# Second-half projections in 512-column passes, with some stores issued by ScalarE

## The chip, the cores and the metric

The kernel runs on one core of one Trainium2 chip. A core has a matrix engine (TensorE, PE in the profile), VectorE (DVE), ScalarE (ACT), GpSimd (POOL) and SyncE (SP). Each has its own instruction queue and works through it in order. In this kernel SP issues every DMA: loads at line 235, stores at line 240. The metric is the device time of one execution in microseconds; the kernel before takes 1905.05 us, the median of three runs (1902.53 to 1905.58).

## The reference

One layer of a streaming encoder works on 2048 prompt frames and 64 sample frames of width 1024. All arithmetic is float32.

```python
h = rmsnorm(x, norm_g) @ w_in            # 1024 -> 6144 columns
qa, ka, va, za, qb, kb, vb, zb, ga, gb = jnp.split(h, _split_points(), axis=-1)
# branch A: differential attention, 4 heads, q and k in two 64-wide halves, 128-wide values
s = einsum(q, k) / 8 - slope * |q_pos - k_pos|, masked to chunks of 64 up to the query's own
p = softmax(s);  a = p[:, :, 0] - lam * p[:, :, 1];  oa = a @ v
# branch B: retention, 4 heads, 128-wide, a decaying state carried from chunk to chunk
o = (q k^T * decay inside the chunk) v + q r * decay;  r = decay_c * r + k^T v * zeta
# merge
m = ga * ((rmsnorm(oa) * silu(za)) @ w_oa) + gb * ((rmsnorm(ob) * silu(zb)) @ w_ob)
y = x + m @ w_out
```

The outputs are y, the normalised attention keys, the attention values and the final retention states. The sample frames run the same layer against a cache of 4096 past frames.

## The kernel before

**Precision.** Each float32 operand is split into a high part, rounded to TensorE's fp32r type, and a low part, the rest. A product takes three fp32r matmuls: high by high, high by low, low by high. ScalarE makes the high part by a copy, POOL or VectorE the low part by a subtraction.

**Two halves of the prompt.** The projection runs first over frames 0 to 1023 and the sample frames, then over frames 1024 to 2047 (`half` 0 and 1). Its parts come in two kinds. A *natural* part (`natural`) keeps a tile of 128 frames stationary and streams weight columns past it; the output has frames in its partitions. The queries, keys and values of attention (`qa`, `ka`, `va`) and the values of retention (`vb`) are made so. A *transposed* part (`transposed`) keeps 128 weight columns stationary and streams frames. Retention's queries and keys (`qb`, `kb`) and the gates (`za`, `zb`, `ga`, `gb`) are made so, in the first half by a seven-product Strassen scheme (`strassen`, line 848). All plain projection matmuls stand in `mm_group`, line 998.

**Wide and narrow.** In the first half the natural parts take 512 weight columns at once (`wide`): 8 pieces of 128 x 512. In the second half each takes two passes of 256 columns: 4 pieces of 128 x 2 x 256 a pass, and two frame tiles share one PSUM bank of 512 columns. A piece is staged in a `ws` buffer, cast by ScalarE (line 952) and its low part taken by POOL (line 962); high and low parts sit in 12 places of tag `w`, each 128 x 512 floats.

**After each group** a finisher takes the bank. `fin_va` has ScalarE cast the high part into `thi` (one buffer, line 1246) and copy the raw values into `ev` (three, line 1248), and VectorE make the low part in `tlo` (two, line 1250); the three are stored. `fin_qk` normalises, transposes on PE and stores. `fin_vb` copies and stores. `fin_t`, for a transposed group, copies into `ev` and calls `put`, which stores. Every store goes through `st` and so to SP's queue.

**Order of the work.** A planner in the kernel's own Python runs generators as tasks. Each has a priority and yields the time at which it can go on, by a cost model (`P`, `A`, `V`, `G`, `ld`, `st`). When PE is free in the model the first ready task in order of priority issues its next instructions. The program order of TensorE, ScalarE and VectorE is the order so made. Attention and retention (`z_stream`) come before the projection (`w_stream`), which fills what they leave.

In the second half the parts come in this order before the change: first pass of va, of ka, of qa, a mark `kqv0`, the second passes, a mark `kqv1`, vb in two passes, then qb and kb in two units each, a mark `ret`, then the gates. While they run, attention works on the first half and then, its loads allowed by the marks, on the second. Per pair of query blocks it makes scores (`qk_block`, matmuls at lines 1517 and 1518, VectorE's bias and minimum at 1526), exponentials (ScalarE, 1557), the difference (VectorE, 1579), and then transposes the weights (1629), splits them (1642, 1644) and multiplies by the values (1607 to 1609). Scores lie in a row arena, one tile of `LATER` = 12032 columns for both halves, which retention shares. `load_head` and `load_q` issue the loads of keys, values and queries.

When both streams are done the output stage runs: branch projections (line 2306 on) and the final product (line 2430 on). Its weights and gated branch outputs are prepared from the moment attention ends.

Of the kernel before, what the change touches and what calls it, by code (L numbers as in the profile page):

```python
# [39 lines left out]
LAT = 250.0  # L40
SLACK = 400.0
# [8 lines left out]
LATER = 12032  # L50
# [38 lines left out]

class Arena:  # L90
    def __init__(self, tile, n):
        self.tile = tile
        self.at = [0.0] * (n // GRAIN)
        self.turn = 0

# [9 lines left out]
    def place(self, sizes, now):  # L105
        got = []
        for n in sizes:
            k = -(-n // GRAIN)
            best = None
            for a, b in self.runs():  # L110
                for x in (a, b - k):
                    if b - a >= k:
                        cost = max(now, max(self.at[x:x + k])), b - a
                        if best is None or cost < best[0]:
                            best = cost, x
            if best is None:
# [7 lines left out]
        return [Span(self.tile[:, a * GRAIN:a * GRAIN + n], a, n) for (a, k, w), n in zip(got, sizes)], t  # L124
# [12 lines left out]
class Hybrid:  # L137
# [73 lines left out]

    def has(self, *tags):
        return all(self.res[t].free for t in tags)
# [25 lines left out]
    def st(self, dst, src, nbytes=0):  # L239
        self.nc.sync.dma_start(dst, src)  # L240
        return self.pe + nbytes / 150.0 + DMA_LAT

# [388 lines left out]
    def w_room(self, wide, nw, q):  # L631

        if not wide:
            tags, pool, shape = ("w", "w"), self.wp, [128, 2, 256]
        elif nw in (0, 2):
            tags, pool, shape = ("S", "S"), self.ap, [128, 2, 512]
        else:
            tag, pool = yield from self.w_pair()
            tags, shape = (tag, tag), [128, 1, 512]
# [3 lines left out]
        elif u == 0:  # L643
            for tag in tags:
                yield from self.take(tag)
            self.wroom = [self.sb(pool, shape, tag, n, F32R) for tag, n in zip(tags, ("wh", "wl"))]
# [498 lines left out]
    def rows_out(self, dst, src, nu, nbytes):  # L1145
        if nu == 1:
            return self.st(dst, src, nbytes)
        return self.st(dst.rearrange("(u p) n -> p u n", u=nu), src.rearrange("p (u n) -> p u n", u=nu),
# [84 lines left out]
    def fin_va(self, g, nh=2):  # L1233
# [4 lines left out]
        def fin(ps, r, nu, t0, t, bank="mm"):  # L1238
# [20 lines left out]
            self.give("thi", self.rows_out(self.vN[0][t0:t0 + rt, gsl], hi.bitcast(F32), nu, nh << 16))  # L1259
            yield t2  # L1260
            td = self.rows_out(dst.rearrange("t h e -> t (h e)"), raw, nu, nh << 16)
# [4 lines left out]
            self.give("tlo", self.rows_out(self.vN[1][t0:t0 + rt, gsl], lo.bitcast(F32), nu, nh << 16))  # L1266
# [21 lines left out]
    def transposed(self, half, dst, d0, scale=None, grouped=True):  # L1288
        us = []
        groups = [(0, 0, 512), (1, 0, 256), (1, 256, 320)]  # L1290
        for ct in range(2):
            for k, (seg, col, n) in enumerate(groups):
                yield from self.take("mm")
                ps = self.psum("mm")[:, :n]
                last = ct == 1 and k == len(groups) - 1
# [112 lines left out]

    def attn_tables(self):
# [6 lines left out]
    def load_head(self, half, h):  # L1416
# [84 lines left out]
    def qk_block(self, h, p, b, ks, q, pair):  # L1501
# [6 lines left out]
        for c in range(2):  # L1508
            row = yield from self.grab(nk)
# [34 lines left out]
    def softmax(self, st, nk, b, pair):  # L1544
# [4 lines left out]
        half = nk if nk <= 1280 else (nk // 256) * 128  # L1549
# [26 lines left out]
        for sl in parts:  # L1576
# [5 lines left out]
            self.drop(rows[1], t2, sl.start, sl.stop)  # L1582
# [6 lines left out]
    def at_pv(self, h, p, vs, tv, pair, last_pair):  # L1589
# [27 lines left out]
        for kp in range(nkt // 2):  # L1617
# [15 lines left out]
            for row in arows:  # L1633
                self.drop(row, t, 256 * kp, min(256 * kp + 256, row.n))
# [963 lines left out]
    def w_stream(self):  # L2598
# [3 lines left out]
        fva = [(va + 256 * g, lambda half, g=g, f=f: self.natural(half, self.fin_va(g), f))  # L2602
               for g in range(2) for f in (True, False)]
        fva, fva0 = fva[1::2], fva[0]
        fk = [(ka + 256 * g, lambda half, g=g: self.natural(half, self.fin_qk("k", g))) for g in range(2)]
        fq = [(qa + 256 * g, lambda half, g=g: self.natural(half, self.fin_qk("q", g))) for g in range(2)]
        m0, m1 = (None, "kqv0"), (None, "kqv1")
        self.S, self.sunits, self.sraw, self.seg1_read, self.summed = {}, [], [], None, False
# [24 lines left out]
        seqs = [first[0] + early + seq, first[1] + later + seq]  # L2633
# [42 lines left out]
    def attn_zone(self):  # L2676
# [9 lines left out]
        self.tp_ = self.z1.enter_context(self.tc.tile_pool(name="tmp", bufs=1, side="right"))  # L2686
        self.attn_tables()
# [25 lines left out]
    def run(self):  # L2713
# [19 lines left out]
        self.state = self.wo = None  # L2733
# [36 lines left out]


def ORD(va0, va, k, q, m0, m1):
    return [va0, k[0], q[0], m0, va[1], k[1], q[1], m1]
# [56 lines left out]
```

## Time and profile before

| what | before |
|---|---|
| median of 3 runs | 1905.05 us |
| profiled execution | 1906.88 us |
| its span, first to last instruction | 1904.8 us |
| mean granted TensorE clock | 0.996 |
| PE busy | 1886.2 us (99%) |
| DVE busy | 1277.7 us (67%) |
| ACT busy | 947.4 us (50%) |
| POOL busy | 590.5 us (31%) |
| DMA moved | 313.10 MB, mean 164 GB/s |

A group of instructions is read as: line, engine, operation, output and inputs, shape, count, then busy time in total, mean of one, and the idle time before it with what ended it. A wait is read as: who waited, for whom, us in total, times, the longest. A window gives busy time and count of each engine, then the granted clock, the busy share of the DMA engines and GB/s. Matmuls overlap, so the duration of one is longer than the distance from one start to the next.

### The profile page before, as it was taken

The page shows a single profiled execution, that of the slowest core. Times are in us where ns is not written, and L with a number is a line of the kernel's source. Part 1 is how long each engine was busy: PE and PEld are TensorE (multiplying, and loading weights), DVE is VectorE, ACT ScalarE, POOL GpSimd, SP SyncE. Part 2 cuts the span into 40 slices and gives each one's busy share as a digit, 9 for nine tenths or more (in the row PEclk, how much of TensorE's full clock was granted, in tenths as well). Part 3 has the DMA queues.
Part 4 walks back from the last instruction along what each step waited for, and adds up shares of the span by engine and source line. Part 5 has one row for each costly group of instructions (what it writes and reads, how often), then busy time and mean ns, then how long its engine had stood idle before and what let it go on. Part 6 is the DMA issues. An engine that isn't in the chain of part 4 may idle for free. (4 is left out here: it accounts for less than half of the span.)

```text
span 1904.8 us, 33589 instructions
## 1 busy us (share of the span) xinstructions
PE 1886.2 (99%) x11690; PEld 1691.2 (89%) x11690; DVE 1277.7 (67%) x3058; ACT 947.4 (50%) x2151; POOL 590.5 (31%) x557
## 2 busy tenths in 40 slices
PE   9999999999998999999999999999999999999999
PEld 7788888888887999999999989999999999999887
DVE  6765766657565787777676765676773139987664
ACT  6434554444443556565555565555565335554221
POOL 2420355556541212221111122111113515522442
PEclk9999999999998999999999999999999999999999
DMA  7654555565557848475325347435216548886542
GB/s 255 215 173 132 161 169 176 168 188 186 175 164 212 241 154 223 144 212 142 99 74 149 99 122 202 110 99 146 80 52 187 173 135 244 257 248 204 173 154 79
DMA packets 361323, 313.10 MB, mean 164 GB/s; under 512 B 67905, under 2 KB 319937, under 8 KB 361154
## 3 DMA queue, kind: packets, MB, share of 16 engines
q1 hardware_dynamic: 361154, 310.97, 55.7%
q8 instruction: 92, 1.51, 0.3%
q14 instruction: 77, 0.63, 0.1%
HBM read 205.43 MB, written 104.60 MB: 163 GB/s over the span
## 5 line engine op out<-in xcount | busy, mean ns | idle before, releaser
L962 POOL TENSOR_TENSOR wl<-ws,wh 128x512 fp32r<-128x512 f32 x125 | 171.9, 1389 | 373.5 <-ACT wh L952 326.1
L998 PE MATMUL mm<-xh,wh 128*128 128x512 f32 (+2 forms) x768 | 255.7, 333 | 0.0
L998 PE MATMUL mm<-xl,wh 128*128 128x512 f32 (+2 forms) x768 | 251.5, 327 | 0.0
L998 PE MATMUL mm<-xh,wl 128*128 128x512 f32 (+2 forms) x768 | 251.4, 327 | 0.0
L998 PE MATMUL mm<-wh,xh 128*128 128x256 f32 (+1 forms) x760 | 249.1, 328 | 0.0
L998 PE MATMUL mm<-wh,xl 128*128 128x256 f32 (+1 forms) x760 | 242.5, 319 | 0.0
L998 PE MATMUL mm<-wl,xh 128*128 128x256 f32 (+1 forms) x760 | 242.1, 319 | 0.0
L1644 DVE TENSOR_TENSOR atl<-at,ath 128x512 fp32r<-128x512 f32 (+1 forms) x144 | 93.6, 660 | 111.5 <-ACT ath L1642 110.9
L998 PEld LDWEIGHTS mm<-xh,wh 128*128 128x128 f32 x768 | 144.9, 189 | 11.1
L998 PEld LDWEIGHTS mm<-xl,wh 128*128 128x128 f32 x768 | 145.1, 189 | 10.7
L998 PEld LDWEIGHTS mm<-wh,xh 128*128 128x128 f32 x760 | 144.5, 190 | 11.2 <-DVE raw L1170 0.2
L998 PEld LDWEIGHTS mm<-wl,xh 128*128 128x128 f32 x760 | 144.5, 190 | 10.9
L998 PEld LDWEIGHTS mm<-xh,wl 128*128 128x128 f32 x768 | 144.8, 189 | 10.5
L998 PEld LDWEIGHTS mm<-wh,xl 128*128 128x128 f32 x760 | 144.3, 190 | 10.7
L1557 ACT ACTIVATE row<-row,a_mx 128x896 f32<-128x896 f32 (+5 forms) x144 | 149.3, 1040 | 8.1 <-DVE a_mx L1536 7.9
L1642 ACT CAST ath<-at 128x512 fp32r<-128x512 f32 (+1 forms) x144 | 79.8, 565 | 139.0 <-PE at L1629 138.1
L1399 POOL TENSOR_TENSOR r_y<-r_y,r_sq 128x256 f32<-128x256 f32 x32 | 30.2, 945 | 322.1 <-DVE r_sq L1396 129.6
L727 POOL TENSOR_TENSOR wl<-ws,wh 128x256 fp32r<-128x256 f32 x64 | 57.6, 899 | 193.8 <-ACT wh L718 188.7
L1526 DVE CUSTOM_DVE_ANT_0 row<-s,dfar 128x512 f32<-128x512 f32 (+2 forms) x147 | 90.5, 631 | 26.0 <-PE s L1518 25.4
L1517 PE MATMUL s<-K,q 128*128 128x512 f32 (+3 forms) x244 | 91.8, 378 | 8.1 <-DVE a_acc L1526 8.1
L1579 DVE SCALAR_TENSOR_TENSOR row<-row,a_w 128x896 f32<-128x896 f32 (+6 forms) x88 | 98.0, 1123 | 0.0
L1307 ACT COPY ev<-mm 128x512 f32<-128x512 f32 (+2 forms) x84 | 38.6, 460 | 113.2 <-PE mm L998 105.1
(497 smaller groups left out, 5489.7 us busy)
## 6 DMA issues: line engine op xcount, KB each, us to landing
ws<-in_w_in_dram SPq DMA_DIRECT2D x160, 256.0 KB, 3.2
q<-qT SPq DMA_DIRECT2D x128, 128.0 KB, 3.0
K<-kT SPq DMA_DIRECT2D x48, 256.0 KB, 5.2
V<-vN SPq DMA_DIRECT2D x24, 512.0 KB, 5.1
row<-in_x_prompt_dram SPq DMA_DIRECT2D x16, 512.0 KB, 4.4
wz<-in_w_in_dram SPq DMA_DIRECT2D x32, 256.0 KB, 4.5
row<-in_cache_k_T_dram SPq DMA_DIRECT2D x32, 256.0 KB, 3.6
row<-in_cache_v_diff_dram SPq DMA_DIRECT2D x32, 256.0 KB, 3.1
```

The lines of the kernel that those rows point to most:

```text
L727: nc.gpsimd.tensor_sub(l[:, cs], src, h[:, cs].bitcast(F32))
L962: self.nc.gpsimd.tensor_sub(l, st, h.bitcast(F32))
L998: nc.tensor.matmul(ps, p, q, start=c == 0 and i == 0, stop=c == KC - 1 and i == 2)
L1307: nc.scalar.copy(ev, ps)
L1399: nc.gpsimd.tensor_mul(y, y, sq)
L1517: nc.tensor.matmul(ps, q1s, kk, start=True, stop=False)
L1526: nc.vector.tensor_tensor_reduce(out=row[:, k0:k0 + n], in0=ps, in1=tab, scale=-SLOPES[h], scalar=3.0e38, op0=ALU.add, op1=ALU.min, accum_ ...
L1557: nc.scalar.activation(u, u, AF.Exp, bias=mx, scale=-1.0, accum_out=lp[:, k:k + 1])
L1579: nc.vector.scalar_tensor_tensor(out=u0, in0=u1, scalar=w[:, 0:1], in1=u0, op0=ALU.mult, op1=ALU.add)
L1642: nc.scalar.copy(ah[:, :w], at[:, :w])
L1644: nc.vector.tensor_sub(al[:, :w], at[:, :w], ah[:, :w].bitcast(F32))
```

## The change

The second half's natural parts become wide: 512 columns at once, one frame tile to a bank. The order becomes qb unit 0, va, qb unit 1, ka, kb unit 0, qa, both marks `kqv0` and `kqv1`, kb unit 1, vb, a new mark `nat`, the mark `ret`, the gates. The first transposed part of a half uses four column groups, ordered so that the first ones need only the first frames.

The wide parts need 16 weight places. 4 more come from a pool `spare`, opened with attention's buffers; for this the row arena begins with 9984 columns. After the mark `nat`, once the four places are free, the pool is closed and the arena gets a second tile of 2048 columns (`more_rows`). Rows of over 1280 scores are taken as two spans of 1024 and the rest (`Row`), and the exponentials are cut at 1024.

A new `st_act` issues a store on ScalarE's queue. The stores of the attention values (high, raw, low) for frames 1024 to 2047, and those of retention's queries and keys with `t0 >= 1024`, go that way. The first two query loads and the distance table get pauses between them in the plan. Attention's further query loads wait for the first head's buffers instead of for a flag that is set earlier.

```diff
+ISSUE = 100.0
-LATER = 12032
+LATER = 9984
+MORE = 2048
...
+class Row:
+    def __init__(self, *spans):
+        self.spans = spans
+        self.n = sum(p.n for p in spans)
+    def piece(self, lo, hi):
+        for p in self.spans:
+            if hi <= p.n:
+                return p, lo, hi
+            lo, hi = lo - p.n, hi - p.n
...
+    def st_act(self, dst, src, nbytes=0):
+        self.nc.scalar.dma_start(dst, src)
+        self.act = max(self.act, self.pe) + ISSUE
+        return self.act + nbytes / 150.0 + DMA_LAT
...
         if not wide:
-            tags, pool, shape = ("w", "w"), self.wp, [128, 2, 256]
+            if any(p[0] for p in self.pieces):
+                tag, pool = yield from self.w_pair(4)
+            else:
+                yield from self.take("w", 2)
+                tag, pool = "w", self.wp
+            tags, shape = (tag, tag), [128, 2, 256]
...
-    def w_pair(self):
+    def w_pair(self, nw=0):
+        if nw >= 4 and not self.spare:
+            yield lambda: self.spare or len(self.res["w"].free) >= 2
+        if nw >= 4 and not self.spare:
+            yield from self.take("w", 2)
+            return "w", self.wp
         tag = yield from self.either(2, "w", "wx")
-        return tag, self.wp if tag == "w" else self.first
+        return tag, self.wp if tag == "w" else self.spare or self.first
...
-            self.give("thi", self.rows_out(self.vN[0][t0:t0 + rt, gsl], hi.bitcast(F32), nu, nh << 16))
+            st = self.st_act if 1024 <= t0 < T else self.st
+            self.give("thi", self.rows_out(self.vN[0][t0:t0 + rt, gsl], hi.bitcast(F32), nu, nh << 16, st))
...
         groups = [(0, 0, 512), (1, 0, 256), (1, 256, 320)]
-        for ct in range(2):
-            for k, (seg, col, n) in enumerate(groups):
+        order = [(ct, k) for ct in range(2) for k in range(3)]
+        if self.npart[half] == 0:
+            groups = [(0, 0, 256), (0, 256, 256), (1, 0, 256), (1, 256, 320)]
+            order = [(0, 0), (1, 0), (0, 1), (1, 1), (0, 2), (0, 3), (1, 2), (1, 3)]
...
         if not grouped:
-            t = self.st(dst[:, t0:t0 + npr], ev[:, :npr], 512 * npr)
+            st = self.st_act if t0 >= 1024 else self.st
+            t = st(dst[:, t0:t0 + npr], ev[:, :npr], 512 * npr)
             if n > npr:
-                t = self.st(dst[:, T:TT], ev[:, npr:n], 1 << 16)
+                t = st(dst[:, T:TT], ev[:, npr:n], 1 << 16)
...
+    def more_rows(self):
+        yield lambda: "nat1" in self.done and len(self.res["wx"].free) == 4
+        yield max(self.res["wx"].free)
+        self.zs.close()
+        pool = self.z1.enter_context(self.tc.tile_pool(name="att2", bufs=1, side="right"))
+        self.ar.add(pool.tile([128, MORE], F32, tag="row2", name="row", bufs=1), MORE, self.pe)
...
-            for p in range(2):
-                yield from self.load_q(0, p)
+            yield from self.load_q(0, 0)
+            yield self.pe + 3000
+            yield from self.load_q(0, 1)
+            yield self.pe + 2000
...
-                yield lambda: self.far
+                yield lambda: len(self.heads) > 0 or h or half
...
-            row = yield from self.grab(nk)
+            row = Row(*(yield from self.grab(1024, nk - 1024))) if nk > 1280 else Row((yield from self.grab(nk)))
...
-        first = ([wva, wk, wq, m0, m1], ORD(fva0, fva, fk, fq, m0, m1))
-        later = [(vb + 256 * g, lambda half, g=g: self.natural(half, self.fin_vb(g, 2))) for g in range(2)]
-        seqs = [first[0] + early + seq, first[1] + later + seq]
+        wide = [(va, lambda half: self.natural(half, self.fin_va(0, 4), False, True), True),
+                (ka, lambda half: self.natural(half, self.fin_qk("k", 0, 4), False, True), True),
+                (qa, lambda half: self.natural(half, self.fin_qk("q", 0, 4), False, True), True)]
+        later = [(vb, lambda half: self.natural(half, self.fin_vb(), False, True), True)]
+        seqs = [first + early + seq, [seq[0], wide[0], seq[1], wide[1], seq[2], wide[2], m0, m1, seq[3], *later, (None, "nat"), *seq[4:]]]
```

More of the change, by code (lines that the diff above doesn't have):

```diff
@@ L123, in place @@
         t = max(max(w) for a, k, w in got)
-        return [Span(self.tile[:, a * GRAIN:a * GRAIN + n], a, n) for (a, k, w), n in zip(got, sizes)], t
+        return [Span(self.part(a, n), a, n) for (a, k, w), n in zip(got, sizes)], t
     def drop(self, span, t, lo, hi):
@@ L637, in w_room @@
         else:
[L638 removed]
+            tag, pool = yield from self.w_pair(nw)
             tags, shape = (tag, tag), [128, 1, 512]
@@ L643, in w_room @@
         elif u == 0:
-            for tag in tags:
-                yield from self.take(tag)
+            if wide:
+                yield from self.take("S", 2)
             self.wroom = [self.sb(pool, shape, tag, n, F32R) for tag, n in zip(tags, ("wh", "wl"))]
@@ L1581, in softmax @@
             t2 = self.V(n + 110, t)
-            self.drop(rows[1], t2, sl.start, sl.stop)
+            self.leave(rows[1], t2, sl.start, sl.stop)
             yield self.dve - PACE
@@ L2601, in w_stream @@
         gb = 5120
[L2602 to L2606, printed above, removed]
         m0, m1 = (None, "kqv0"), (None, "kqv1")
+        self.npart = [0, 0]
         self.S, self.sunits, self.sraw, self.seg1_read, self.summed = {}, [], [], None, False
```

48 lines of the change are left out of this document (36 added, 12 removed).

## The prediction

> **What bounds the kernel now.** I read the page first, then the waits of TensorE, then the places that these named in order of time.
>
> ```profile
> span 1904.8 us, 33589 instructions
> PE 1886.2 (99%) x11690; PEld 1691.2 (89%) x11690; DVE 1277.7 (67%) x3058; ACT 947.4 (50%) x2151; POOL 590.5 (31%) x557
> PEclk9999999999998999999999999999999999999999
> ```
>
> TensorE (PE) is busy 1886.2 of 1904.8 us, and the granted clock is below nine tenths in one slice of 40 only (the 13th, about 571 to 619 us). So time goes in two ways alone: less array time per unit of work, or fewer holes. The waits of PE show how few holes there are:
>
> ```profile
> PE s L1517 <- DVE a_acc L1526: 8.1, 2, 7.9
> PE at L2307 <- DVE ogl L2263: 3.1, 3, 2.0
> ```
>
> One hole of 7.9 us carries most of it. It lies where the second half begins; three short windows across it (columns: PE busy and count, weight loads, DVE, ACT, POOL, granted clock, DMA share):
>
> ```profile
> 606.30:614.30 8.00, 0.16 (x2) 0.00 (x0) 0.93 (x4) 1.59 (x4) 0.37 (x1) 0.66 1.04 312
> 614.30:619.16 4.86, 4.84 (x17) 4.48 (x17) 3.15 (x15) 3.85 (x13) 2.25 (x3) 0.50 0.73 220
> 619.16:624.20 5.04, 5.04 (x43) 5.04 (x42) 3.16 (x14) 3.47 (x9) 2.23 (x2) 1.00 0.72 208
> ```
>
> After the hole PE runs 4.84 us at a granted clock of 0.50: half of that, 2.4 us, is lost as well. The hole thus costs 7.9 + 2.4 = 10.3 us. What made it, from the timelines of ScalarE, VectorE and the SP queue:
>
> ```profile
> 596.26 0.59 ACT L1248 COPY raw<-mm 128x512 f32<-128x512 f32 x1
> 612.26 0.59 ACT L1246 CAST thi<-mm 128x512 fp32r<-128x512 f32 x1 [15.41 <-DMA vN<-thi]
> 613.37 0.69 DVE L1250 TENSOR_TENSOR tlo<-mm,thi 128x512 fp32r<-128x512 f32 x1 [15.79 <-ACT raw L1248]
> 613.97 0.28 DVE L1526 CUSTOM_DVE_ANT_0 row<-s,dnear 128x128 f32<-128x128 f32 x1
> ...
> 597.53 6.02 SPq L235 DMA_DIRECT2D q<-qT  x8
> 603.60 0.60 SPq L235 DMA_DIRECT2D dfar<-in_c_dfar_dram  x1
> 604.24 1.06 SPq L235 DMA_DIRECT2D V<-vN  x2
> 605.39 2.43 SPq L240 DMA_DIRECT2D vN<-thi  x1
> ```
>
> The high half of a value tile was cast by 596.3 us. Its store waited on SP behind eight query loads (6.02 us), the distance table and two value loads, was issued at 605.39 and let go of the only `thi` buffer at 612.26. ScalarE stood 15.4 us in front of that buffer, VectorE 15.8 us behind ScalarE, and the first score tiles of attention, queued on VectorE behind L1250, kept PE's banks.
>
> **The change part by part.**
>
> *Wide natural parts.* va, ka, qa and vb of the second half go from two 256-column passes to one of 512: 4 x 2 x 8 row tiles x 8 x 3 = 1536 matmuls of 256 columns (all three forms below) become 768 of 512. Busy times overlap here, so I take the distance from start to start.
>
> ```profile
> L998 PE MATMUL mm<-wh,xh 128*128 128x256 f32 x512 | 149.5, 292 | 0.0
> L998 PE MATMUL mm<-wh,xl 128*128 128x256 f32 x512 | 144.9, 283 | 0.0
> L998 PE MATMUL mm<-wl,xh 128*128 128x256 f32 x512 | 144.8, 283 | 0.0
> 584.00:605.20 21.20, 21.18 (x177) 21.18 (x176) 1.00 0.69 183
> 149.67 0.40 PE L998 MATMUL mm<-wh,xh 128*128 128x512 f32 x1
> 152.24 0.40 PE L998 MATMUL mm<-wh,xl 128*128 128x512 f32 x1
> 1776.00:1824.00 48.00, 48.00 (x208) 38.92 (x208) 26.96 (x35) 12.18 (x21) 20.09 (x13) 1.00 0.50 157
> ```
>
> A stretch of nothing but 256-column matmuls gives 21.2/177 = 0.1198 us. The same natural form at 512 columns, in the first half, runs 11 distances in 2.57 us: 0.2336. The last stage, all 512, runs 48/208 = 0.2308. Two for one: 0.2396 - 0.2336 = 6.0 ns or 0.2396 - 0.2308 = 8.8 ns, times 768: 4.6 to 6.8 us. I take 5.5, a little nearer to the row of the same form.
>
> The Trainium skill (TensorE: Matmul & The Clock Gate, Back-to-back issue gap) gives a warm matmul N/2.4 ns and a fixed 2.5 ns more. By that estimate halving the count would save 768 x 2.5 ns = 1.9 us and no more; the rows here have 13 ns above the 106.7 ns of 256 columns.
>
> *The first retention unit in four column groups.* In both its column tiles one group of 512 becomes two of 256: 48 matmuls become 96, 48 x 8.8 ns = 0.4 us lost. It lets the unit start on the first 256 columns of x, as the narrow value part did; I cost the start at nothing, since the work per 256 columns (48 matmuls) is the same as before.
>
> *Order.* Retention's units now lie between the wide parts, and both marks that let attention of the second half load come after three wide parts and three units, not after three and six narrow passes. On PE's path this adds nothing while other work fills it; the price if not is the slower rival below.
>
> *Stores on ScalarE.* For the prompt's second half 8 x 3 = 24 value stores and 8 per retention unit plus 2 for the first, 34, move from SP to ScalarE: 58 issues. ScalarE issues no DMA before, so the price is bounded by the same stores on SP:
>
> ```profile
> L240 SPq DMA_DIRECT2D vN<-thi x17: 326/383/2431, 18.4 to 730.0; - x17
> L240 SPq DMA_DIRECT2D vN<-tlo x17: 319/437/865, 21.3 to 732.0; - x17
> L240 SPq DMA_DIRECT2D kbT<-ev x24: 319/338/1243, 280.1 to 1074.2; - x24
> 576.00:888.00 312.00, 303.69 (x2436) 297.42 (x2435) 235.49 (x687) 176.99 (x439) 58.58 (x48) 0.98 0.67 191
> ```
>
> At about 0.39 us each, 58 issues are 23 us of ScalarE where it has 177 of 312 us busy; the ends are 0 and 58 x 2.4 = 139 us, and the medians speak for the low side. Behind an issue stand evictions, the exponentials and the `ath` casts, for which PE waits. But a hold of 15.4 us became 7.9 us of hole, so the plan has some 7.5 us of slack, three times the longest issue (2.43). I cost this at nothing on PE. The last of three value stores makes ScalarE wait for VectorE's subtraction (0.69 us), under the same slack.
>
> What the move takes away is the hole: the `thi` store no longer stands behind query loads, and when attention starts PE is in a retention unit, whose evictions use three `ev` buffers and no `thi`. I take the whole 10.3 us. If half the lateness stayed, 4 us of hole would stay too; none of it gone is the lower end. What is late next at that place is the landing itself: 605.39 to 612.26 is 6.9 us at a DMA share near 1. Cast at 596.3 and issued at once, the store would land near 603.2, inside the slack.
>
> The Trainium skill (DMA: Bandwidth & Descriptors, Issuing engines are not separate DMA queues) says that all issuing engines share 16 DMA engines, and a second issuer saves sequencer time only. The trace agrees so far as 9 of the 15.4 us were spent before the issue; by that rule the 6.9 us would remain, which the sentence before allows for.
>
> *Weights and buffers at no cost on PE.* A wide part needs 8 weight pairs, all 16 places; while a narrow unit holds 8, four pairs can wait ready, and POOL makes the other four as the unit's last group lets go. Cover gone, 8 pairs cost POOL more than PE takes to use them in its first row tile:
>
> ```profile
> L962 POOL TENSOR_TENSOR wl<-ws,wh 128x512 fp32r<-128x512 f32 x125 | 171.9, 1389 | 373.5 <-ACT wh L952 326.1
> ```
>
> 8 x 1.389 = 11.1 us against 24 x 0.2336 = 5.6: 5.5 us at each of four meetings, 22 us at most. Key and query stores go in pieces of 512 bytes instead of 1 KB, off PE's path. The row arena is 9984 columns for a while instead of 12032; its cost is that of a later attention.
>
> *Sum.* 1906.9 us (the profiled execution; 2.1 outside its span) - 10.3 - 5.5 + 0.4 = 1891.5. That execution is 1.8 us above the median of 1905.05, so on the median's level 1889.7: about 1890.
>
> **The rivals.** *Slower: attention's tail.* The projections are the filler that keeps PE full beside attention; a later attention could outlast them.
>
> ```profile
> L1629 PE MATMUL at<-ident,row x544: 270/272/277, 625.8 to 1432.9; 128*128 128x128 f32 x182
> L998 PE MATMUL mm<-xh,wh x768: 277/309/482, 894.1 to 1545.0; 128*128 128x512 f32 x64, 128*128 128x256 f32 x64, 128*128 128x320 f32 x64
> L1517 PE MATMUL s<-K,q x36: 277/389/497, 926.5 to 998.8; 128*128 128x512 f32 x28, 128*128 128x256 f32 x5, 128*128 128x384 f32 x3
> 576.00:888.00 312.00, 203.28 (x1495) 190.01 (x1496) 0.98 0.67 191
> 1440.00:1536.00 96.00, 96.00 (x583) 88.10 (x582) 1.00 0.60 174
> 883.67 2.38 SPq L235 DMA_DIRECT2D K<-kT  x4
> 912.00:1440.00 528.00, 293.80 (x1584) 244.76 (x1585) 1.00 0.41 112
> ```
>
> Attention's last transposes start at 1432.9, the last projection at 1545: 112 us of cushion, shortened by the 15 saved to 97. The marks now come after 3 x 192 x 0.2336 + 3 x 144 x 96/583 = 135 + 71 = 206 us of projection. By 888 us the old order had done 1495 matmuls, 1495 x 0.1198 = 179; with the hole gone 189, so the marks fall near 905, and 9 us of planned waiting more puts the key loads at 914, where they began at 883.7: attention starts up to 30 us after its old 926. The smaller arena may add to it. It decides from a slip of about 97 us; beyond that PE has only attention, and 1584 x 96/583 = 261 of 528 us were filler, so each further us costs about half. A slip of 150 us gives 1890 + 0.5 x 53 = 1917, and with the output stage's preparation uncovered some 1920. For it: up to 30 us is worked out, the arena's part unknown. Against: 67 us are left.
>
> *A new hole takes the old one's place* (ScalarE held by an issue on full queues, or `thi` late again in a wide part): the 10.3 stays, 1905 - 5.1 = 1900.
>
> *The wide parts bring little* (1.9 instead of 5.5, the hole still gone): 1893, inside the likeliest range.
>
> *Weights late* at most meetings, 15 us: 1905, no change.
>
> **How the numbers follow.** Likeliest 1890 (own range 1884 to 1896): 0.54, with 1893 another 0.08; new hole 1900: 0.14; weights late 1905: 0.07; tail 1920: 0.15; better than 1884: 0.02. Under 0.2% (3.8 us) a measurement of this kernel hardly tells from no change. Faster 0.78, same 0.07, slower 0.15. From 1884 to 1904 lie 0.54 + 0.08 + 0.14 and part of the 0.07, some 0.8.
>
> **What would show it.** Right: no wait of PE on L1526 near 606 us, no clock of 0.5 there, 768 natural matmuls of 512 columns at 0.231 to 0.234 us, the last projection near 1529 and attention's last transposes before 1500. Wrong: a PE wait above 5 us on a ScalarE result whose ScalarE wait ends on a DMA or an issue; PE idle at the start of wide parts on L962; L1629 ending after L998.

## The result, and the profile after

The changed kernel takes 1896.9 us (median of 8 runs, 1895.18 to 1901.83). The kernel before, run beside it, takes 1903.49 us (8 runs, 1902.19 to 1905.58). The ratio is 0.9968, with a 95% interval of 0.9958 to 0.9979: 6.6 us or 0.3% faster. Beside the later experiments the kernel before had medians of 1904.59 to 1905.01 us, so 6.6 may be at the low end of what the change is worth. The forecast was a gain of 15 us, so the direction holds and the size does not, though 1896.9 lies inside the range of 1884 to 1904. The profiled execution of the changed kernel took 1897.25 us.

Lines 998, 848, 1517, 1526 and 1629 of before are 1044, 894, 1583, 1592 and 1695 of after. SP issues loads at line 266 and stores at 271, ScalarE its stores at 275. The page of the kernel after:

```profile
span 1895.5 us, 32119 instructions
PE 1878.8 (99%) x10970; PEld 1651.5 (87%) x10970; DVE 1288.1 (68%) x3058; ACT 947.4 (50%) x2153; POOL 587.2 (31%) x557
PEclk9999999999999999999999999999999999999999
```

11690 matmuls became 10970: 768 fewer by the wide parts and 48 more by the four column groups, as worked out. The waits of TensorE in the kernel after (who waited, for whom, us in total, times, longest):

```profile
PE at L2374 <- DVE ogl L2330: 2.7, 2, 2.0
PE s L1584 <- DMA q<-qT: 2.3, 2, 1.9
PE s L1583 <- DMA q<-qT: 1.4, 1, 1.4
```

The 7.9 us on VectorE's bias is gone. In its place PE now waits for the query loads themselves. Windows of the kernel after over the same place (PE busy and count, weight loads, DVE, ACT, POOL, granted clock, DMA share, GB/s):

```profile
600.00:604.00 4.00, 2.83 (x21) 2.63 (x20) 0.00 (x0) 0.43 (x1) 0.00 (x0) 1.00 1.04 248
604.00:606.30 2.30, 0.30 (x1) 0.19 (x1) 0.00 (x0) 0.00 (x0) 0.00 (x0) 0.69 0.52 148
606.30:611.70 5.40, 5.34 (x24) 5.37 (x25) 1.82 (x11) 2.35 (x9) 0.00 (x0) 0.50 0.83 266
584.00:660.00 76.00, 71.68 (x464) 65.62 (x463) 47.75 (x134) 38.30 (x94) 11.84 (x10) 0.96 0.78 227
```

PE stands 1.2 us before 604 and 2.0 us after, and then runs 5.4 us at a clock of 0.50: the picture of before, with shorter gaps (3.2 us against 7.9) and a slow stretch that is no shorter (5.4 us against 4.84). The two first score matmuls and what ended the idle time before them, from PE's timeline (start, us, then the instruction), and SP's timeline beside it. The last line is the first score matmul of the kernel before, which waited for nothing:

```profile
604.21 0.30 PE L1583 MATMUL s<-K,q 128*128 128x128 f32 x1 [1.38 <-DMA q<-qT]
606.36 0.45 PE L1584 MATMUL s<-K,q 128*128 128x128 f32 x1 [1.85 <-DMA q<-qT]
...
595.19 2.39 SPq L266 DMA_DIRECT2D K<-kT  x4
597.63 6.56 SPq L266 DMA_DIRECT2D q<-qT  x4
...
605.25 0.22 PE L1517 MATMUL s<-K,q 128*128 128x128 f32 x1
```

PE came to the scores at 602.8 us, 2.4 us earlier than before, and the queries were not there; its instructions for the scores were next in its own order, so it stood until the loads landed. From SP's first query load to the end of the fourth lie 6.56 us, where before eight took 6.02. The loads themselves were not slow; the issue times of the four (ns, min, median, max) and what SP waited for between them:

```profile
L266 SPq DMA_DIRECT2D q<-qT x4: 573/586/603, 597.6 to 603.6; - x4
SPq L266 <- DMA qbT<-ev: 2.5, 1, 2.5
SPq L266 <- DMA K<-kT: 1.6, 2, 0.9
```

Each issue took 0.57 to 0.60 us. In between SP stood 4.1 us: twice until a key load had landed, and for 2.5 us until one of ScalarE's stores (`qbT`) had. In the kernel before the waits among the eight were 1.0 us, on key loads alone.

**Where the time went.** To compare executions I cut each span into windows of 2 us. In a window the idle time is 2 minus PE's busy time, and where the granted clock is under 0.99 the busy time times (1 - clock) counts as lost too. What is left of the span is called the array's own time. All in us; the experiments below are in the same table, named by their labels.

| profiled execution | span | lost to 584 | 584 to 660 | 660 to 1500 | from 1500 | array |
|---|---|---|---|---|---|---|
| before | 1904.8 | 3.1 | 10.3 | 0.7 | 8.6 | 1882.2 |
| before again (e5) | 1902.6 | 2.9 | 11.2 | 1.2 | 4.9 | 1882.4 |
| after | 1895.5 | 3.1 | 7.1 | 1.9 | 7.3 | 1876.1 |
| after again (e6) | 1894.2 | 2.6 | 6.9 | 1.0 | 6.4 | 1877.4 |
| e1, stores on SP | 1898.6 | 3.0 | 6.3 | 1.5 | 10.1 | 1877.8 |
| e2, old order, stores on ScalarE | 1903.5 | 4.6 | 7.3 | 2.9 | 4.8 | 1883.9 |
| e3, first pair 6 us later | 1894.0 | 2.6 | 8.8 | 1.1 | 5.1 | 1876.4 |
| e4, e3 with narrow parts | 1909.2 | 3.0 | 8.7 | 5.3 | 7.3 | 1884.9 |
| e7, long pauses | 1906.7 | 4.1 | 10.6 | 8.1 | 5.2 | 1878.7 |
| e8, no pauses | 1901.1 | 2.5 | 10.0 | 1.4 | 9.5 | 1877.6 |
| e9, e3 with stores on SP | 1894.9 | 2.6 | 7.3 | 1.7 | 6.4 | 1876.9 |
| e10, first pair 12 us later | 1904.3 | 3.6 | 12.1 | 2.9 | 8.8 | 1876.8 |
| e11, e3 with queries on GpSimd | 1896.1 | 2.5 | 8.3 | 0.7 | 7.9 | 1876.7 |
| e12, e3 without tables and values | 1889.8 | 2.6 | 3.0 | 1.0 | 6.9 | 1876.4 |

Between the two first profiles the array's time fell by 6.1 us and the hole's by 3.2. The prediction had 5.1 (5.5 less 0.4) and 10.3. The column from 1500 us (the output stage) differs by 3.7 us between two executions of the same kernel before, so single profiles say nothing about it.

### The profile page after: what moved, and what is told of

It reads as the page before. It is cut to its first block, busy times and chain, and to the rows that moved or that the text cites. A ratio compares the mean times of both kernels' runs of the same rounds, so it can differ in the third digit from the quotient of the medians.

```text
span 1895.5 us, 32119 instructions
## 1 busy us (share of the span) xinstructions
PE 1878.8 (99%) x10970; PEld 1651.5 (87%) x10970; DVE 1288.1 (68%) x3058; ACT 947.4 (50%) x2153; POOL 587.2 (31%) x557
## 4 chain that ended last, share of the span: by engine, by line
PE 91%; DMA 3%; DVE 3%; ACT 1%; issue 1%; POOL 1%; SPq 0%; DVEq 0%; POOLq 0%; ACTq 0%
PE mm L1044 35%; PE mm L894 9%; PE tp L894 5%; PE at L1695 3%; PE s L1584 3%; PE s L1583 3%; PE s L894 2%; PE pv L1675 2%; PE pv L1674 2%; PE pv L1673 2%; PE s L2499 1%; PE s L2498 1%; PE s L2497 1%; PE pv L1961 1%; PE at L2064 1%
## 5 line engine op out<-in xcount | busy, mean ns | idle before, releaser
L1044 PE MATMUL mm<-xh,wh 128*128 128x256 f32 (+2 forms) x784 | 260.2, 332 | 0.0
L1044 PE MATMUL mm<-xh,wl 128*128 128x256 f32 (+2 forms) x784 | 254.9, 325 | 0.0
L1044 PE MATMUL mm<-xl,wh 128*128 128x256 f32 (+2 forms) x784 | 254.9, 325 | 0.0
L1044 PE MATMUL mm<-wh,xh 128*128 128x512 f32 x504 | 203.2, 403 | 0.0
L1044 PE MATMUL mm<-wl,xh 128*128 128x512 f32 x504 | 197.5, 392 | 0.8 <-POOL wl L1008 0.8
L1044 PE MATMUL mm<-wh,xl 128*128 128x512 f32 x504 | 197.8, 392 | 0.0
L1044 PEld LDWEIGHTS mm<-xh,wh 128*128 128x128 f32 x784 | 148.9, 190 | 10.1
L1623 ACT ACTIVATE row<-row,a_mx 128x1024 f32<-128x1024 f32 (+7 forms) x144 | 149.7, 1042 | 12.2 <-DVE a_mx L1602 12.1
L1044 PEld LDWEIGHTS mm<-wh,xl 128*128 128x128 f32 x504 | 94.6, 188 | 21.4
L1044 PEld LDWEIGHTS mm<-wh,xh 128*128 128x128 f32 x504 | 94.8, 188 | 17.2 <-DVE raw L1217 0.2
L1645 DVE SCALAR_TENSOR_TENSOR row<-row,a_w 128x1024 f32<-128x1024 f32 (+5 forms) x88 | 97.7, 1116 | 0.0
```

The source lines that it names most:

```text
L1044: nc.tensor.matmul(ps, p, q, start=c == 0 and i == 0, stop=c == KC - 1 and i == 2)
L1623: nc.scalar.activation(u, u, AF.Exp, bias=mx, scale=-1.0, accum_out=lp[:, k:k + 1])
L1645: nc.vector.scalar_tensor_tensor(out=u0, in0=u1, scalar=w[:, 0:1], in1=u0, op0=ALU.mult, op1=ALU.add)
```

## The experiments

The question was why a hole of some 7 us stayed where one of 10 had gone, and what each part of the change is worth.

**e1: the stores back on SP.** The new order, without ScalarE's issues:

```diff
-            st = self.st_act if 1024 <= t0 < T else self.st
+            st = self.st
...
-            st = self.st_act if t0 >= 1024 else self.st
+            st = self.st
```

> The changed kernel with its value, query and key stores put back on SP; wide parts and order as changed. Theory A (the new hole is a plan that starts attention some 3 us before its queries land; the issuing engine has little to do with it): PE still waits near 604 us on a query load, some 3 us and as much again at half clock, and the evictions behind SP may add to it: 1897 to 1903 us. Theory B (stores on ScalarE's queue run beside the query loads on the same DMA engines and hold these up): the four query loads are issued at some 0.6 us each again instead of 1.6, PE's wait on them goes, 5.9 us less than the changed kernel: about 1891 us.

Measured: 1899.06 us (1898.22 to 1900.39) against 1905.01, ratio 0.9970, interval 0.9958 to 0.9981; the whole change has 0.9968. The waits of PE from 584 to 660 us in e1, and SP's issue of the first four query loads there:

```profile
PE s L1583 <- DVE a_acc L1592: 2.4, 1, 2.4
PE s L1583 <- DMA q<-qT: 1.1, 1, 1.1
PE s L1584 <- DMA q<-qT: 1.0, 2, 0.8
...
598.24 2.56 SPq L266 DMA_DIRECT2D q<-qT  x4
```

With the stores on SP the four query loads are issued in 2.56 us instead of 6.56, so SP's standing between them does come with the stores on ScalarE's queue. It isn't what makes the hole: the first score starts no earlier (604.49 us against 604.21), PE waits as long in all, half of it now on VectorE's bias, and the loss is 6.3 us against 7.1 and 6.9. The time lies where theory A had it.

**e2: the stores alone.** The kernel before, with `st_act` and its two choices, and nothing else of the change:

```diff
+            st = self.st_act if 1024 <= t0 < T else self.st
...
+            st = self.st_act if t0 >= 1024 else self.st
```

> The kernel before, in its old order with narrow passes, with only the stores of values and of retention's queries and keys of the second half issued by ScalarE. The prediction's step (a thi store stuck behind query loads on SP makes the hole of 7.9 us and 2.4 us of half clock): the hole goes, 10.3 us less than before: about 1893 us. Rival (in an ordinary execution the hole is smaller than in the profiled one, which was 3.4 us above the median of eight): 5 to 7 us less: 1897 to 1899 us. Rival (a query wait takes its place at once): 1899 to 1903 us.

Measured: 1902.48 us against 1905.01, ratio 0.9989, interval 0.9981 to 0.9998. PE's waits there (lines 1525 and 1526 are the scores of this kernel):

```profile
PE s L1525 <- DMA q<-qT: 2.7, 1, 2.7
PE s L1526 <- DMA q<-qT: 1.9, 2, 1.3
```

The mechanism of the prediction is confirmed and is not enough. With the `thi` stores off SP the wait of 7.9 us on the bias is gone, in the old order of work too; 4.6 us on queries take its place, as the second rival had it, and the loss falls from 10.3 and 11.2 to 7.3. Part of that lateness comes with the move itself: among these query loads SP stood 4.0 us until a ScalarE store (`vN<-tlo`) had landed, and the eight were issued in 9.08 us instead of 6.02.

**e3: the first pair of query blocks planned 6 us later.** The new kernel, where the plan is told that the first two query loads arrive 6 us after its own estimate:

```diff
-        self.qs.append((q, t))
+        self.qs.append((q, t + 6000 if h == 0 and p < 2 else t))
```

> The changed kernel; in the plan the first two query blocks of attention count as landed 6 us later, so that other work is put in front of the first scores; nothing else. Theory A (PE's waits on query loads near 604 us, 3.2 us, and the half clock after them, 2.7 us, are where most of the missing gain is): no PE wait on q near 604, clock 1.00 between 600 and 612, 5.9 us less than the changed kernel: about 1891 us. Rival (the hole moves to the next late thing, values or tables): within 1.5 us of the changed kernel, 1895 to 1898.

Measured: 1895.84 us (1894.56 to 1896.63) against 1905.01, ratio 0.9951, interval 0.9939 to 0.9964. PE's waits from 584 to 660 us in e3, then ScalarE's longest from 600 to 640:

```profile
PE s L1583 <- DVE a_acc L1592: 2.5, 1, 2.5
PE mm L1044 <- ACT wh L998: 2.0, 1, 2.0
PE mm L1044 <- POOL wl L1008: 0.6, 1, 0.6
...
ACT wh L998 <- DMA ws<-in_w_in_dram: 9.8, 3, 4.2
```

No wait on queries is left, but the hole has only moved, to 613 to 624 us: PE now does projection while it waits for queries, uses up its weights, and the next ones are late. The loss is 8.8 us, 3.8 of it at half clock, and the time is the rival's. It is the fastest version that computes everything; its interval overlaps that of the change as it stands.

**e4: narrow parts in the new order.** e3, with va, ka, qa and vb of the second half in two 256-column passes at the same places in the order.

```diff
+        wide = [[(c0 + 256 * g, lambda half, g=g, f=f: self.natural(half, f(g))) for g in range(2)]
+                for c0, f in ((va, self.fin_va), (ka, lambda g: self.fin_qk("k", g)), (qa, lambda g: self.fin_qk("q", g)))]
...
-        later = [(vb, lambda half: self.natural(half, self.fin_vb(), False, True), True)]
+        later = [(vb + 256 * g, lambda half, g=g: self.natural(half, self.fin_vb(g, 2))) for g in range(2)]
```

> As e3_first_pair_later, but va, ka, qa and vb of the second half in two narrow passes each, at the same places of the order. The prediction's term (two matmuls of 256 columns take 6.0 to 8.8 ns longer than one of 512): 4.6 to 6.8 us slower than e3_first_pair_later: about 1896 to 1898 us if that is 1891. The skill's 2.5 ns a matmul: 1.9 us slower. Rival (wide parts bring waits of their own on weights or on thi): no slower, or faster.

Measured: 1911.54 us (1910.24 to 1912.86) against 1905.01, ratio 1.0033, interval 1.0021 to 1.0045: 15.7 us more than e3, over twice the 6.8 that the prediction's term allows, so that with narrow parts the new order is slower than the kernel before. The array's time is 8.5 of it (1884.9 less 1876.4). Over 768 pairs that is 11 ns for a pair. The kernel before has the same narrow parts in its own order; against it the wide parts gained 6.1 and 5.0 us net of some 0.4 for the column groups, which is 7.0 to 8.5 ns for a pair. What adds the rest in e4's order isn't shown. The spans differ by 15.2 us; besides the array's 8.5, 4.2 are lost between 660 and 1500 us and 2.2 in the output stage. At the opening e4 loses 8.7 us, as much as e3, by one wait on queries:

```profile
PE tp L1583 <- DMA q<-qT: 5.3, 1, 5.3
```

The same 45 us of the two kernels, e3's kind of part first in the kernel after, then in e4:

```profile
900.00:945.00 45.00, 45.00 (x250) 39.11 (x249) 21.09 (x45) 18.50 (x42) 11.70 (x10) 1.00 0.59 177
```

```profile
900.00:945.00 45.00, 45.00 (x359) 43.98 (x358) 24.14 (x58) 22.81 (x54) 11.74 (x10) 1.00 0.55 167
```

PE is full in both. In the narrow kernel the weight loads (the second pair of numbers) fill the stretch as well, 43.98 of 45 us; in the wide one they leave 6 us.

**e5 and e6: both kernels again.** One more profile of each, unchanged, to see whether the holes belong to the programs.

> The kernel before once more, unchanged, for a second profiled execution. If the hole near 606 us belongs to the program, it costs 10.3 us again (idle time plus time lost at half clock between 584 and 660 us). If it depends on how the transfers of one execution fall, it differs by some us: 5 to 8 us would put the prediction's profiled run at the costly end.

> The changed kernel once more, unchanged. Hole between 584 and 660 us 7.1 us in the first profile; the program's own: within 1 us of that; by the fall of the transfers: anywhere from 3 to 10.

Measured: before 1904.52 us, after 1895.97. Before's wait from 584 to 660 us:

```profile
PE s L1517 <- DVE a_acc L1526: 9.7, 1, 9.7
```

The losses are 11.2 and 6.9 us, and the array's times 1882.4 and 1877.4. Both holes are the programs' own; the array's gain is 5.0 here and 6.1 in the first pair.

**e7 and e8: the pauses of the plan longer, and none.** e7 makes the pauses between the opening loads 6 and 8 us instead of 3 and 2 and doubles the one ahead of head 1; e8 takes out the two. e7's diff, then e8's:

```diff
-            yield self.pe + 3000
+            yield self.pe + 6000
...
-            yield self.pe + 2000
+            yield self.pe + 8000
...
-                yield self.pe + CALM
+                yield self.pe + 2 * CALM
```

```diff
             yield from self.load_q(0, 0)
-            yield self.pe + 3000
             yield from self.load_q(0, 1)
-            yield self.pe + 2000
             self.ld(self.dfar, self.i["c_dfar"], 1 << 19)
```

> The changed kernel with attention's opening loads spread out in the plan: 6 and 8 us of pause instead of 3 and 2 between query loads, distance table and first values, and the second head's keys and values 36 instead of 18 us after the first. Theory A2 (after the second half begins, attention's opening asks for more than the transfers deliver in that time; whatever stands behind on SP's queue is late, and PE waits for one or another of these): the loss between 584 and 660 us falls from 7.1 to under 3 us: 4 to 5 us faster than the changed kernel, about 1892 us. Rival (the hole only moves to the next late thing, as it did when the first pair was put off): within 1.5 us of the changed kernel.

> The changed kernel without the two pauses (query loads, distance table and values in one go, as before the change). Theory A2: more asked for at once, the loss between 584 and 660 us grows by 1 to 3 us: 1898 to 1900 us where the changed kernel has 1896.9. Rival (the pauses do nothing, since SP is still busy with the first queries when they end): the same within 1 us.

Measured: e7 1908.46 us (1905.27 to 1910.36) against 1904.59, ratio 1.0017, interval 1.0008 to 1.0026. e8 1903.57 us (1898.77 to 1906.45) against 1904.59, ratio 0.9994, interval 0.9985 to 1.0003. PE's waits from 584 to 660 us in e8:

```profile
PE s L1581 <- DMA q<-qT: 3.6, 2, 2.3
PE s L1582 <- DMA q<-qT: 3.3, 3, 2.3
```

Without the pauses the loss is 10.0 us, as large as the old hole, with queries as its cause. So the two pauses, to which the prediction gave no term, carry much of what the change gains: 6.7 us lie between the medians of e8 and of the change, measured beside different runs of before; by the ratios it is 0.26%, 5 us. For e8 theory A2 had the direction, and the rival falls. Longer pauses lose too: 10.6 us at the opening and 6.2 us more than the change from 660 to 1500. Both sides of e7 missed, A2 by its sign; what the pause ahead of head 1 did in it was not tested by itself.

**e9: e3 with the stores on SP.** The edits of e1 and e3 together:

```diff
-            st = self.st_act if 1024 <= t0 < T else self.st
+            st = self.st
...
-        self.qs.append((q, t))
+        self.qs.append((q, t + 6000 if h == 0 and p < 2 else t))
```

> First pair of query blocks planned 6 us later, and all stores back on SP. Theory of the queue (SP's slow issue of the query loads beside ScalarE's stores keeps the weights behind them late): the four query loads issue in about 2.6 us instead of 6.4, the three weight loads near 611 us no longer take 5 us, and the loss from 584 to 660 us falls from 8.8 to under 5: 1892. Theory of the shared transfers (the same bytes have to land in the same stretch, whoever issues them): the loss stays between 6 and 10 us and the time at 1894 to 1898, as with the stores on ScalarE.

Measured: 1898.59 us (1896.85 to 1904.41) against 1904.73, ratio 0.9973, interval 0.9963 to 0.9984. The four query loads were issued in 2.55 us, as both theories had it, and the loss is 7.3 us, as only that of the shared transfers had it; the time is 0.6 us above its upper end. The wait on weights went, one of 3.5 us on the bias came. Three pairs now tell what ScalarE's stores are worth: 2.5 us alone (e2), 2.2 in the new order (e1 beside the change; by the ratios, each with its own runs of before, 0.4) and 2.8 in e3's (e9; by the ratios 4.2). All three have the same sign, but in the new order as it stands nothing is shown.

**e10: the first pair 12 us later.** e3 with the larger delay:

```diff
-        self.qs.append((q, t + 6000 if h == 0 and p < 2 else t))
+        self.qs.append((q, t + 12000 if h == 0 and p < 2 else t))
```

> First pair of query blocks planned 12 us later instead of 6. If the hole is only the plan's optimism about when the first loads land, 12 us is more than the lateness seen (some 8 us): no wait on queries or on VectorE's bias above 1 us, loss from 584 to 660 us under 4: 1890 to 1892. If the projection's own weights are late behind the opening's loads, the waits on weights (about 3.5 us at 613 to 624 us with 6 us) stay or grow, and the time is that of the 6 us version, 1895 to 1897.

Measured: 1905.46 us (1902.21 to 1908.61) against 1904.73, ratio 1.0003, interval 0.9994 to 1.0012. PE's waits from 584 to 660 us:

```profile
PE mm L1044 <- ACT wh L998: 5.5, 2, 4.2
PE s L2040 <- DMA row<-kbT: 1.8, 1, 1.8
PE mm L1044 <- POOL wl L1008: 1.4, 2, 0.9
```

Waiting longer for queries costs the weights more: 5.5 us on `wh` against 2.0, a loss of 12.1 and a time 8 us above what either side expected. The plan's date of the first pair alone isn't the cause.

**e11: the query loads of the first head's first half issued by GpSimd.** On top of e3, so that no weight load stands behind a query load on SP.

```diff
+                t = self.ld(..., 1 << 17, self.nc.gpsimd if h == 0 and p < 4 else None)
...
+        (eng or self.nc.sync).dma_start(dst, src)
```

> First pair planned 6 us later, and the query loads of the first head's first half issued by GpSimd instead of SP, so that the weight loads stand behind no query load on SP. Theory of the queue: the weight loads are issued without delay, the waits on weights (3.5 us) go, loss from 584 to 660 us under 5: 1891 to 1893. Theory of the shared transfers: the weights are issued earlier but land no earlier, the loss stays at 6 to 10 us: 1895 to 1898. Against both: GpSimd makes the weights' low parts, and an issue of 1.6 us or more there delays them; then waits on the low part grow and the time is 1896 to 1900.

Measured: 1896.52 us (1895.27 to 1897.88) against 1904.73, ratio 0.9957, interval 0.9940 to 0.9974; the loss is 8.3 us. PE's longest wait there, and the three weight loads (tile `ws`) behind the values: count, issue time (ns, min, median, max), first and last start, and the time from the start of the issue to landing. The same two lines of e3's three loads stand in the second fence.

```profile
PE mm L1044 <- ACT wh L998: 3.8, 1, 3.8
...
L266 SPq DMA_DIRECT2D ws<-in_w_in_dram x3: 405/541/4594, 608.4 to 613.6; - x3
DMA to landing us min/median/max: 9.3/9.9/12.3
```

```profile
L266 SPq DMA_DIRECT2D ws<-in_w_in_dram x3: 402/419/3970, 611.4 to 615.9; - x3
DMA to landing us min/median/max: 5.9/6.4/9.1
```

These three were issued 2.3 to 2.9 us earlier than in e3 and landed 0.2 to 1.2 us later (at 620.70, 622.39 and 623.50 us against 620.49, 621.37 and 622.31). What the queue gave, the transfers took back. The theory of the queue falls. GpSimd issued a query load in 0.6 us, not 1.6, and PE's wait on the low part stayed at 0.6 us.

**e12: the opening with fewer bytes.** On top of e3, the distance table and the first head's two value tiles of the first half are set to zero by VectorE instead of loaded. The far bias and that head's outputs for the first half are left out, and 1.5 MB of transfers with them.

```diff
-            self.ld(self.dfar, self.i["c_dfar"], 1 << 19)
+            self.nc.vector.memset(self.dfar, 0.0)
...
+                if half == h == 0:
+                    self.nc.vector.memset(v.bitcast(F32), 0.0)
```

> First pair planned 6 us later; the distance table and the first head's two value tiles for the first half aren't loaded but set to zero by VectorE (idle in that stretch), so the far bias and that head's outputs for the first half are left out. That takes 1.5 MB of transfers (some 6 us at the 237 to 285 GB/s of the stretch) out of 600 to 620 us and costs VectorE some 3 us there. Theory of the shared transfers: the weight loads behind them land some 5 us earlier, the waits on weights (3.5 us) go, the loss from 584 to 660 us falls from 8.8 to 3 to 5: 1889 to 1892. If the loss lies in the plan alone (too little other work put between the first scores), the loss stays at 7 to 10 us wherever it falls: 1894 to 1898.

Measured: 1890.89 us (1889.06 to 1891.57) against 1904.68, ratio 0.9928, interval 0.9911 to 0.9944. PE's waits from 584 to 660 us, the six weight loads from 595 to 625 us, and the window:

```profile
PE s L1588 <- DVE a_acc L1597: 2.0, 1, 2.0
PE s L1589 <- DMA q<-qT: 0.6, 1, 0.6
PE s L1588 <- DMA q<-qT: 0.5, 1, 0.5
...
L266 SPq DMA_DIRECT2D ws<-in_w_in_dram x6: 373/386/992, 604.8 to 618.0; - x6
DMA to landing us min/median/max: 2.8/3.7/3.8
...
584.00:660.00 76.00, 73.01 (x467) 65.92 (x466) 48.87 (x144) 36.76 (x91) 10.23 (x8) 1.00 0.83 227
```

The weights land in 3.7 us in the median, where e3's six took 5.9; every wait on them is gone, the clock stays at 1.00, and the loss falls from 8.8 to 3.0 us. Of these 5.8 us, 3.8 are half clock that no longer follows. The time falls by 5.0 us against e3 (4.4 by the ratios), at an array time of 1876.4 in both. The plan is not the difference: from 600 to 660 us PE has the same instructions in the same order in both. So in e3's order most of the loss is the price of bringing the opening's transfers in (keys, queries, table, values and the projection's own weights) between 595 and 625 us. The edit takes out three loads along with their bytes and doesn't tell the two apart. That the 7 us of the change as it stands have the same cause is inferred: fewer bytes were not tried there. Who waits is a matter of order: VectorE's bias behind a `thi` store in the old kernel, queries in the new one, weights in e3.

## Why the prediction was right or wrong

**The hole: the step that failed.** "I take the whole 10.3 us." The cause named there was right: the wait on the bias at 606 us has gone, in e2 too, by moving the stores alone. The other sign named for that place, no clock of 0.5, failed. What was named as late next was wrong. The prediction took "the landing itself" of the `thi` store, some 603 us, as the only thing left in that stretch, and found it inside the slack. It didn't ask when the queries themselves would land, although its own rows had eight query loads issued on SP from 597.53 for 6.02 us, and a DMA share of 1.04 right behind them. In the kernel before PE came to the scores at 605.25 us and the queries were there; in the new order it came at 602.8, and the queries let the first score start at 604.21 and the next at 606.36. Measured: 10.3 and 11.2 us of loss became 7.1 and 6.9, a gain of 3 to 4 us instead of 10.3.

Its rival "a new hole takes the old one's place" had the right kind of outcome and the wrong mechanism and place: it looked at ScalarE's issues and at `thi`. Its 1900 is 3 us from the result, the likeliest case's 1890 is 7.

**The wide parts: right.** 5.5 less 0.4 was forecast; the array's time fell by 6.1 and 5.0 us. That is 7.0 to 8.5 ns for a pair, inside the 6.0 to 8.8 taken from stretches of nothing but one width; only in e4's order is it 11 ns. The rival "the wide parts bring little" is contradicted by these runs. Its 1.9 us came from the Trainium skill (TensorE: Matmul & The Clock Gate, Back-to-back issue gap), which gives the 2.5 ns for the gap of an isolated matmul and says that in a stream of weight loads and matmuls both set the spacing; here each matmul has its weight load.

**ScalarE's issues: right.** They were costed at nothing on PE, at about 0.39 us each. The stores on ScalarE in the kernel after (min, median, max in ns):

```profile
L275 ACTq DMA_DIRECT2D qbT<-ev x18: 326/326/464, 587.2 to 760.4; - x18
L275 ACTq DMA_DIRECT2D vN<-tlo x8: 326/327/491, 629.2 to 703.8; - x8
```

58 issues at 0.33 us are 19 us of ScalarE, none over 0.5 us. The rival of a ScalarE held by full queues did not come. What was missed is the other queue: SP's loads now wait for these stores to land, 2.5 us ahead of the fourth query load in the change and 4.0 us in e2. In the new order that is not what the hole hangs on: with the stores on SP (e1) the loss is 6.3 us.

**The shared transfers: the rule was cited and not followed.** The Trainium skill (DMA: Bandwidth & Descriptors, Issuing engines are not separate DMA queues) has all issuers share 16 DMA engines. The prediction applied it to the one store that it had in view. e11 shows it at work on the weights in that stretch: issued 2.3 to 2.9 us earlier, landed 0.2 to 1.2 us later.

**The pauses: no term.** The prediction's part by part has no line for the pauses in the plan, and e8 says 5 us. It counted "9 us of planned waiting" for the tail, from the marks, but not the two pauses of the opening.

**The tail: right in size.** The last transposes of attention and the last projections in the kernel after:

```profile
L1695 PE MATMUL at<-ident,row x544: 270/272/329, 618.0 to 1462.2; 128*128 128x128 f32 x182
L1044 PE MATMUL mm<-xh,wl x784: 278/309/415, 583.9 to 1537.0; 128*128 128x256 f32 x72, 128*128 128x320 f32 x64, 128*128 128x512 f32 x60
```

Attention slipped from 1432.9 to 1462.2, 29 us, inside the "up to 30" worked out; 75 us of cushion stayed. The slower rival did not happen. The size was met by another route than the one worked out: the key loads at that place of the sequence, which the prediction put at 914 instead of 883.67, begin at 859.20, and yet the scores after them start at 951.1 instead of 926.5. What held the scores was not looked for, so the match with "up to 30" is in part luck.

**Weights at no cost: right in the change as it stands**, where the longest wait on the low part is 0.8 us; in e3 and e10 weights became the bound, by late landing and not by POOL's 1.389 us.

**The level.** The profiled execution of before was taken as 1.8 us above the median, of three runs. Against eight runs it is 3.4 above (1906.88 less 1903.49), and that of after 0.4 above: between the two profiles lie 9.6 us, between the medians 6.6. The sum with the measured terms, 1906.9 - 3.2 (hole) - 6.1 (array) = 1897.6, comes near the profiled execution of after (1897.25) because the other columns cancel (1.2 worse, 1.3 better). So of the 15.4 us forecast, 7.1 are missing in the hole, and another 3.0 are the level: the two profiles lie that much further apart than the medians.

## What to carry to other kernels

When a wait is taken away, list everything that must land in the same stretch, with its bytes, and work out when each would be there, not only what stood behind the removed wait; here, with a DMA share near 1 in the stretch, moving issues to another queue shifted the lateness to the next tile, and fewer bytes took it away (1.5 MB less were worth 5 us, a queue of their own nothing). Before calling an issue slow, read what its queue waited for between the issues. A program that writes its own order by estimated arrival times is sensitive to a few microseconds both ways: no pauses, 5 us of planned ones and 14 us gave ratios of 0.9994, 0.9968 and 1.0017 (the last with another pause doubled as well). Price a tile's width in the order in which it will run: the same narrow parts cost 7.0 to 8.5 ns more for a pair in the old order and 11 in the new one.

## What the hardware showed that was not expected

- SP's loads can stand behind ScalarE's stores. Four query loads of 128 KB were spread over 6.56 us with stores on ScalarE's queue (6.35 in e3, 6.56 in e12) and over 2.56 us with all stores on SP (e1; 2.55 in e9). Each issue took 0.6 us; ahead of the fourth SP waited 2.5 us for a ScalarE store to land (2.7 in e3 and e12). What in the program ties the one to the other was not looked for.
- Two gaps of 1.38 and 1.85 us within 4 us were followed by 5.4 us at a clock of 0.50, as the single gap of 7.9 us was before. A gap of 1.96 us by itself in e12 was followed by none. The time lost to the clock does not go with the length of the gap: 2.8 us here, 2.4 and 1.5 in the two executions of before, after gaps of 7.9 and 9.7.
- Halving the width of 768 matmuls cost 6.0 to 8.8 ns for a pair by stretches of one width, 7.0 to 8.5 ns in the second half of the kernel before, and 11 ns (8.5 us) in e4's order, where weight loads fill 43.98 of 45 us.
- The output stage from 1500 us lost 8.6 us in one execution of the kernel before and 4.9 in another. It is the largest scatter between executions; its cause was not looked for.
